# Column tiles for three groups of small products, and a new price for 64-column tile products in the order of issue

## The chip, the cores and the metric

The kernel runs on one core of one Trainium2 chip. The metric is the device time of one execution in microseconds (us). The kernel before took 1555.84 us, the median of three runs between 1552.79 and 1557.61. On this core five engines work side by side, each through its own list of instructions in a fixed order: TensorE (PE: products, with a weight load, PEld, ahead of each), VectorE (DVE), ScalarE (ACT), GpSimd (POOL) and SyncE (SP), which here only issues transfers (DMAs).

## The reference

One layer of a hybrid decoder is computed for a prompt of 1024 tokens and for 8 single-token samples with the same weights:

```
p = x @ w_in                                  # 1024 -> 9360 columns: GLA, RWKV and gate parts
GLA, 4 heads:   S_t = diag(a_t) S_(t-1) + k_t^T v_t ;   o_t = q_t S_t
RWKV, 16 heads: S_t = S_(t-1) (diag(w_t) - kk_t^T (kk_t a_t)) + v_t^T k_t ;   y_t = S_t r_t
m = sigmoid(gate_a) * (o_gla @ w_up_gla) + sigmoid(gate_b) * (o_rwkv @ w_up_rwkv)
y = layernorm(2^(1/4) x + m @ w_out)
```

The decay `w` and the rate `a` of the RWKV part come from small low-rank products (`rwkv_w2`, `rwkv_a2`, 64 rows each). Outputs are y, the new GLA and RWKV states and the last row before the token shift, for prompt and samples, all in float32.

## The kernel before

**Passes and tiles.** The prompt goes in two passes of 512 tokens; the 8 samples ride along with the first pass, as 8 further columns. Activations lie with their feature on the 128 partitions and their token along the free axis. The large products (`x @ w_in`, the two up-projections, the output) are made from a float32 value split into a high and a low part, so that each block of 128x128 weights costs three products (`xh,whi`, `xl,whi`, `xh,wlo` in the profile). All other products take float32 operands; the profile shows each of those as two matmul records on PE, the two passes of one float32 product (a group of four products is an "x8").

**Pairs and heads.** The 16 RWKV heads go two at a time (8 pairs a pass, function `pair`): `front` makes the factors and the Gram products (`pY<-az,wide` and `big<-az,wide`, 64x64 tiles), `back` completes a blockwise inverse from the tiles `Lp`, `As` and `Xs`, `turn` transposes, `chain` goes through 8 chunks and ends with two groups of 16 products into `pY`. The 4 GLA heads go one after the other (`gla_head`). In the first pass each head also does the samples (`gla_sample`): it loads the 8 states of 128x256 two at a time, updates them on ACT and DVE, stores them, and multiplies each with its sample's query, which stands in one column of an otherwise empty 8-column block (`qm`). `lora_sample` makes the low-rank products of the samples once, near the start.

**What sets the order.** Each such function is a stream of operations. `Order.run` takes, over and over, the operation with the smallest key: the time at which it could start by the planner's own account, less a bonus by the kind of stream (`ON_PE` for products, `PRIO` otherwise). That account adds up a price for each operation (`price`), 0.115 us where the tile shape on PE changes (`SWITCH`), and delays between engines. So a price in that table moves instructions of all engines, though no price is a time on the chip. `tiles` rounds the rows and columns of a product's weights up to 32, 64 or 128; `price` uses both. Everything is recorded through one helper, so that nearly all instructions carry line L219 in the profile, and groups are told apart by tile names and shapes.

**The lines around the change.** In `back` the two groups of 4 products read 128x128 weights and move 32 columns. In `gla_sample` there are 16 products a head, each with a 128x128 half of a state as weights and 8 moving columns:

```
yield self.P.matmul(po[:, j], Sg[:, w, j * P:(j + 1) * P], qm[:, NS * b:NS * b + NS],
                    start=(b == j == 0), stop=(b == NS - 1 and j == 1))
```

In `lora_sample` 4 products of 64 rows, 8 weight columns and 512 moving columns follow one another, each with its own load, bank of PSUM, copy and store. PSUM banks come from pools; `big` has three.

Of the kernel before, what the change touches and what calls it, by code (L numbers as in the profile page):

```python
# [76 lines left out]
PRIO = {"evacuate": 0.7, "pair": 0.4, "gram": 0.4, "turn": 0.5, "chain": 0.5, "norm": 0.1, "x": 0.7, "lora": 0.2, "rank": -0.3,  # L77
        "head": 0.3, "gate": 0.05, "w": 0.3, "out": -0.1, "state": 0, "block": 0.0}
ON_PE = {"evacuate": 0.0, "pair": 0.0, "gram": 0.16, "turn": 0.0, "chain": 0.0, "norm": 0.0, "x": 0.0, "lora": 0.175, "rank": 0.125,
# [67 lines left out]
def price(eng, name, out, args, ins):  # L147
# [3 lines left out]
    if eng == "P":  # L151
# [4 lines left out]
        if args[0].dtype == F32R:  # L156
            return max(m / 1200, n / 2200) if rows == P else (m + n) / 1200
        if rows == cols == P:
            return 2 * max(m, n) / 1200 + 0.005
        return 2 * max(m, n) / 1200 * rows * cols / P ** 2  # L160
# [252 lines left out]
class Kern(Order):  # L413
# [521 lines left out]
    def gla_sample(self, h, q, k, v, al, bufs, qm_):  # L935
# [12 lines left out]
        qm = qm_[:, :NS * NS]  # L948
        yield E.memset(qm, 0.0)
        yield E.tensor_copy(qm[:, ::NS + 1], q[:, HT:])  # L950
# [10 lines left out]
        po = yield from self.bank("big", [P, 2, NS])  # L961
        for n in range(NS // W):
            Sg, vb = (x[:, :W * GDV].rearrange("p (b v) -> p b v", b=W) for x in bufs[n % 2])
            for w in range(W):
                b = n * W + w
                t = HT + b
                yield A.activation(vb[:, w], vb[:, w], AF.Copy, scale=k[:, t:t + 1])
                yield V.scalar_tensor_tensor(Sg[:, w], Sg[:, w], al[:, t:t + 1], vb[:, w], ALU.mult, ALU.add)
                for j in range(2):
                    yield self.P.matmul(po[:, j], Sg[:, w, j * P:(j + 1) * P], qm[:, NS * b:NS * b + NS],  # L970
                                        start=(b == j == 0), stop=(b == NS - 1 and j == 1))
            yield self.S.dma_start(self.o["gla_s"][0, n * W:n * W + W, h].rearrange("b k v -> k b v"), Sg)
            if n + 2 < NS // W:
                yield from load(n + 2)
        for j in range(2):
            yield self.C.copy(v[j][:, HT:], po[:, j])
        self.free(po)
# [21 lines left out]
    def lora_sample(self, lw):  # L999
        for q in range(2):  # L1000
            rs = slice(64 * q, 64 * q + 64)
            for hf in range(2):
                l2, wa = yield from self.rows(2, 512)
                wa8 = wa[:NS]
# [202 lines left out]
    def back(self, d):  # L1207
# [10 lines left out]
        for y in range(NCH // 2):  # L1218
            yield self.P.matmul(pA[:, y], d.Lp[:, y], X1[:, y], start=True, stop=True)
# [554 lines left out]
```

## Time and profile before

| | |
|---|---|
| median of the runs | 1555.84 us (1552.79 to 1557.61) |
| the profiled execution | 1556.64 us, its span from first to last instruction 1554.9 us |
| instructions | 32217 |
| PE busy | 1510.2 us, 97% of the span |
| weight loads (PEld) busy | 1333.8 us, 86% |
| DVE, ACT, POOL busy | 1140.2 us (73%), 875.8 us (56%), 101.2 us (7%) |
| mean granted clock of PE | 0.988 |

A group of the profile is one line, engine, operation, pair of tile names and shape. `64*8` ahead of a matmul's shape are the rows and columns of its weights, and the last number before `f32` counts its moving columns. In a timeline the first column is the start, the second the time from the first start to the last end of the merged records. Matmul records overlap, since the next one enters while the last one still drains; what a product costs is therefore read from one start to the next, not from its own duration.

### The profile page before, as it was taken

What the parts mean: (1) busy time and instruction counts of PE and PEld (TensorE: products, weight loads), DVE (VectorE), ACT (ScalarE), POOL (GpSimd) and SP (SyncE); (2) the same over time, 40 slices, a digit from 0 to 9 for tenths busy, and PEclk for the clock granted to TensorE, in tenths of its full rate; (3) what the DMA queues carried; (4) which work ended last, traced back from release to release, by engine and by line L of the source; (5) the groups of instructions that cost most, each with busy time, mean ns of one, the idle gap of its engine ahead of it and who ended that gap; (6) DMA issues with size and microseconds to landing.
All of it is one profiled execution on the core that took longest, in us unless ns stands there. A gap on an engine that the chain in (4) does not pass through costs nothing.

```text
span 1554.9 us, 32217 instructions
## 1 busy us (share of the span) xinstructions
PE 1510.2 (97%) x11144; PEld 1333.8 (86%) x11144; DVE 1140.2 (73%) x3026; ACT 875.8 (56%) x2230; POOL 101.2 (7%) x208
## 2 busy tenths in 40 slices
PE   8999989999989999999999999999999999999998
PEld 8899979899989899788787778777887799988786
DVE  5695769785879678967877878787786784566665
ACT  5556566756676658664755474556445755554310
POOL 0100000100010001010100000102100000000000
PEclk9999979999999999999999999999999999999999
DMA  9878958678877787657557456855674687798622
GB/s 295 251 223 269 306 152 274 182 219 256 278 207 250 201 290 228 210 160 215 185 157 219 150 154 206 242 145 171 193 225 130 210 241 224 228 296 271 221 90 82
DMA packets 377055, 330.67 MB, mean 213 GB/s; under 512 B 131219, under 2 KB 262428, under 8 KB 376892
## 3 DMA queue, kind: packets, MB, share of 16 engines
q1 hardware_dynamic: 376892, 328.60, 69.7%
q8 instruction: 89, 1.46, 0.4%
q14 instruction: 74, 0.61, 0.1%
HBM read 198.35 MB, written 118.61 MB: 204 GB/s over the span
## 4 chain that ended last, share of the span: by engine, by line
PE 78%; DVE 11%; DMA 5%; ACT 3%; issue 2%; SPq 1%; POOL 0%; POOLq 0%; DVEq 0%; ACTq 0%
PE proj L219 47%; PE big L219 18%; PE pY L219 9%; DVE row L219 5%; PE pch L219 4%; ACT row L219 2%; DVE wide L219 1%; DVE Xt L219 1%; DVE X L219 1%; DMA S<-GS 1%; ACT L392 1%; SPq L219 1%; DMA wide<-LD 1%; DMA az<-wide 1%; DMA whi<-wh 1%
## 5 line engine op out<-in xcount | busy, mean ns | idle before, releaser
L219 PE MATMUL proj<-xh,whi 128*128 128x256 f32 (+2 forms) x1864 | 613.6, 329 | 2.9 <-ACT row L219 2.0
L219 PE MATMUL proj<-xh,wlo 128*128 128x256 f32 (+2 forms) x1864 | 612.4, 329 | 0.6 <-DMA wlo<-wl 0.5
L219 PE MATMUL proj<-xl,whi 128*128 128x256 f32 (+2 forms) x1864 | 612.7, 329 | 0.0
L219 PEld LDWEIGHTS proj<-xh,whi 128*128 128x128 f32 x1864 | 354.2, 190 | 25.4 <-ACT row L219 3.0
L219 PEld LDWEIGHTS proj<-xh,wlo 128*128 128x128 f32 x1864 | 354.6, 190 | 24.5 <-DMA wlo<-wl 1.8
L219 PEld LDWEIGHTS proj<-xl,whi 128*128 128x128 f32 x1864 | 354.4, 190 | 22.3 <-issue 2.2
L219 DVE TENSOR_TENSOR wlo<-wraw,whi 128x512 fp32r<-128x512 f32 x206 | 142.8, 694 | 75.7 <-ACT whi L219 73.6
L219 ACT CAST whi<-wraw 128x512 fp32r<-128x512 f32 x210 | 130.0, 621 | 76.6 <-PE proj L219 19.7
L219 DVE TENSOR_TENSOR row<-row 128x256 f32<-128x256 f32 (+9 forms) x328 | 158.1, 491 | 12.0 <-DMA row<-state_rwkv 3.7
L219 ACT ACTIVATE row<-row 128x512 f32<-128x512 f32 (+3 forms) x229 | 138.6, 611 | 30.9 <-DVE row L219 19.7
L219 DVE TENSOR_TENSOR Xt<-X,wide 128x60 f32<-128x60 f32 (+24 forms) x496 | 106.2, 214 | 23.2 <-DMA wide<-LD 10.6
L219 DVE TENSOR_TENSOR X<-X,Xt 128x60 f32<-128x60 f32 (+24 forms) x496 | 108.0, 218 | 12.5
L219 PE MATMUL big<-row 128*128 128x128 f32 (+3 forms) x530 | 99.7, 295 | 5.7 <-DVE row L219 5.1
L219 POOL TENSOR_TENSOR row<-row 128x512 f32<-128x512 f32 (+6 forms) x57 | 60.9, 1072 | 649.6 <-DVE row L219 296.7
L219 ACT COPY rh<-pch 128x128 f32<-128x128 f32 x114 | 30.5, 268 | 121.3 <-PE pch L219 120.6
L219 ACT ACTIVATE row<-proj,omu 128x256 f32<-128x256 f32 (+1 forms) x99 | 54.1, 547 | 75.1 <-PE proj L219 74.4
L219 DVE SCALAR_TENSOR_TENSOR row<-proj,pv,row 128x255 f32<-128x255 f32 (+1 forms) x99 | 56.5, 571 | 49.8 <-ACT tail L219 31.3
L219 DVE SCALAR_TENSOR_TENSOR wide<-pch,pc,s0p 64x64 f32<-64x64 f32 x224 | 63.1, 282 | 40.1 <-PE pch L219 34.7
L219 PEld LDWEIGHTS big<-row 128*128 128x128 f32 (+1 forms) x530 | 76.7, 192 | 16.3 <-DVE row L219 5.9
L219 ACT ACTIVATE s0p<-wide,pc 64x64 f32<-64x64 f32 x256 | 89.0, 348 | 2.0
L392 ACT ACT_TABLE_LOAD x56 | 71.8, 1283 | 1.0
L219 ACT COPY row<-big 128x128 f32<-128x128 f32 (+5 forms) x149 | 41.9, 303 | 47.1 <-PE big L219 45.9
(280 smaller groups left out, 2537.0 us busy)
## 6 DMA issues: line engine op xcount, KB each, us to landing
wraw<-w_in SPq DMA_DIRECT2D x146, 256.0 KB
wh<-whi SPq DMA_DIRECT2D x146, 256.0 KB
wl<-wlo SPq DMA_DIRECT2D x146, 256.0 KB
whi<-wh SPq DMA_DIRECT2D x146, 256.0 KB
wlo<-wl SPq DMA_DIRECT2D x146, 256.0 KB
wide<-LD SPq DMA_DIRECT2D x64, 128.0 KB
wraw<-w_up_gla SPq DMA_DIRECT2D x32, 256.0 KB
wraw<-w_up_rwkv SPq DMA_DIRECT2D x32, 256.0 KB
```

Source lines behind the costliest of these rows:

```text
L219: ways.append((eng, lambda call=call: call(out, *args, **kw), price(eng, name, out, args, ins)))
L392: self.nc.scalar.preload_act_table_set(self.table)
```

## The change

Three groups of products are rewritten so that they run in tiles of fewer weight columns that stand beside one another in the array, and the prices are changed.

- `back`: each product with 128x128 weights becomes two with 128x64 weights, one for each half of the output partitions. 4 products become 8, twice a pair, 16 pairs. The stream calls itself "gram" meanwhile (bonus 0.16 on PE, where "turn" has none).
- `gla_sample`: weights and moving operand change places. The weights are now 32 columns of `qm` (the sample's query and 31 zeros), the moving operand is a whole state of 256 columns. Four samples go to the four 32-partition quarters of one bank, in two groups a head, 8 products a head instead of 16. The result is the transpose of the one before, so it is copied out of PSUM, transposed by four products a head and copied again. The four state updates and both stores of a group now come before its products, and the second four samples are loaded after the first group's products, where before each two were replaced as soon as they were done.
- `lora_sample`: all loads come first, then the four products together, in two row halves and two column quarters and in two banks that are held at the same time; copies and stores follow.
- `price`: a float32 tile product with at most 64 moving columns is priced by the larger side of its tile and no longer by its area; a product of the split kind (float32r) with all 128 rows is priced in proportion to its weight columns, which lowers the price of the 32-column products at the start of each pass and of one 64-column block at the end. The bonuses have a new kind, "tiles".

```diff
--- before.py
+++ after.py
@@ -74,9 +74,9 @@
 BIAS = 0.1
 ASIDE = 0.5
 
-PRIO = {"evacuate": 0.7, "pair": 0.4, "gram": 0.4, "turn": 0.5, "chain": 0.5, "norm": 0.1, "x": 0.7, "lora": 0.2, "rank": -0.3,
+PRIO = {"evacuate": 0.7, "pair": 0.4, "gram": 0.4, "tiles": 0.3, "turn": 0.5, "chain": 0.5, "norm": 0.1, "x": 0.7, "lora": 0.2, "rank": -0.3,
         "head": 0.3, "gate": 0.05, "w": 0.3, "out": -0.1, "state": 0, "block": 0.0}
-ON_PE = {"evacuate": 0.0, "pair": 0.0, "gram": 0.16, "turn": 0.0, "chain": 0.0, "norm": 0.0, "x": 0.0, "lora": 0.175, "rank": 0.125,
+ON_PE = {"evacuate": 0.0, "pair": 0.0, "gram": 0.16, "tiles": 0.16, "turn": 0.0, "chain": 0.0, "norm": 0.0, "x": 0.0, "lora": 0.175, "rank": 0.125,
          "head": 0.1, "gate": 0.06, "w": 0.0, "out": -0.03, "state": 0.125, "block": 0.0}
 
 URGENT = 0.6
@@ -154,10 +154,10 @@
         if name == "transpose":
             return 0.112
         if args[0].dtype == F32R:
-            return max(m / 1200, n / 2200) if rows == P else (m + n) / 1200
+            return max(m / 1200, n / 2200) * cols / P if rows == P else (m + n) / 1200
         if rows == cols == P:
             return 2 * max(m, n) / 1200 + 0.005
-        return 2 * max(m, n) / 1200 * rows * cols / P ** 2
+        return 2 * max(m, n) / 1200 * (max(rows, cols) / P if n <= 64 else rows * cols / P ** 2)
     if eng == "S":
         return 0.48
     if eng == "A":
@@ -945,9 +945,9 @@
         yield self.S.dma_start(vd, vs)
         self.free(vs_)
 
-        qm = qm_[:, :NS * NS]
+        qm = qm_[:, :NS * 32]
         yield E.memset(qm, 0.0)
-        yield E.tensor_copy(qm[:, ::NS + 1], q[:, HT:])
+        yield E.tensor_copy(qm[:, ::32], q[:, HT:])
         W = 2
 
         def load(n):
@@ -958,23 +958,35 @@
             yield self.S.dma_start(vb[:, :W * GDV], vd[b].rearrange("b v -> (b v)").partition_broadcast(P))
         yield from load(0)
         yield from load(1)
-        po = yield from self.bank("big", [P, 2, NS])
-        for n in range(NS // W):
-            Sg, vb = (x[:, :W * GDV].rearrange("p (b v) -> p b v", b=W) for x in bufs[n % 2])
-            for w in range(W):
-                b = n * W + w
-                t = HT + b
-                yield A.activation(vb[:, w], vb[:, w], AF.Copy, scale=k[:, t:t + 1])
-                yield V.scalar_tensor_tensor(Sg[:, w], Sg[:, w], al[:, t:t + 1], vb[:, w], ALU.mult, ALU.add)
-                for j in range(2):
-                    yield self.P.matmul(po[:, j], Sg[:, w, j * P:(j + 1) * P], qm[:, NS * b:NS * b + NS],
-                                        start=(b == j == 0), stop=(b == NS - 1 and j == 1))
-            yield self.S.dma_start(self.o["gla_s"][0, n * W:n * W + W, h].rearrange("b k v -> k b v"), Sg)
-            if n + 2 < NS // W:
-                yield from load(n + 2)
+        po = yield from self.bank("big", [P, 2, GDV])
+        for g in range(2):
+            for n in range(2 * g, 2 * g + 2):
+                Sg, vb = (x[:, :W * GDV].rearrange("p (b v) -> p b v", b=W) for x in bufs[n % 2])
+                for w in range(W):
+                    t = HT + n * W + w
+                    yield A.activation(vb[:, w], vb[:, w], AF.Copy, scale=k[:, t:t + 1])
+                    yield V.scalar_tensor_tensor(Sg[:, w], Sg[:, w], al[:, t:t + 1], vb[:, w], ALU.mult, ALU.add)
+                yield self.S.dma_start(self.o["gla_s"][0, n * W:n * W + W, h].rearrange("b k v -> k b v"), Sg)
+            yield "tiles"
+            for c in range(4):
+                Sg = bufs[c // W][0][:, :W * GDV].rearrange("p (b v) -> p b v", b=W)
+                yield self.P.matmul(po[QS[c], g], qm[:, 32 * (4 * g + c):32 * (4 * g + c) + 32], Sg[:, c % W],
+                                    start=(g == 0), stop=(g == 1))
+            yield "head"
+            if g == 0:
+                yield from load(2)
+                yield from load(3)
+        os_ = yield from self.row(2 * GDV)
+        yield A.copy(os_, po.rearrange("p g v -> p (g v)"))
+        self.free(po)
+        pt = yield from self.bank("big", [P, 2, 2, P])
+        for g in range(2):
+            for j in range(2):
+                yield self.tr(pt[:, j, g], os_[:, g * GDV + j * P:g * GDV + (j + 1) * P])
+        self.free(os_)
         for j in range(2):
-            yield self.C.copy(v[j][:, HT:], po[:, j])
-        self.free(po)
+            yield self.C.copy(v[j][:, HT:].rearrange("p (g c) -> p g c", g=2), pt[:, j, :, ::32])
+        self.free(pt)
 
 
     def lora(self, c):
@@ -997,18 +1009,23 @@
         self.spawn(parts(), "lora")
 
     def lora_sample(self, lw):
+        l2 = yield from self.rows(2, 512)
+        for hf in range(2):
+            for q, rs in enumerate(HS):
+                yield self.S.dma_start(l2[hf][rs], self.a["lora2"][rs, q, 512 * hf:512 * hf + 512])
+        pw = [(yield from self.bank("big", [P, 512])), (yield from self.bank("big", [P, 512]))]
+        yield "tiles"
+        for hf in range(2):
+            for q, rs in enumerate(HS):
+                yield self.P.matmul(pw[q][32 * hf:32 * hf + NS], lw[rs, HT:], l2[hf][rs], start=True, stop=True)
+        yield "lora"
+        self.free(*l2)
         for q in range(2):
-            rs = slice(64 * q, 64 * q + 64)
+            wa = yield from self.row(2 * HT // 2)
             for hf in range(2):
-                l2, wa = yield from self.rows(2, 512)
-                wa8 = wa[:NS]
-                yield self.S.dma_start(l2[rs], self.a["lora2"][rs, q, 512 * hf:512 * hf + 512])
-                pw = yield from self.bank("big", [NS, 512])
-                yield self.P.matmul(pw, lw[rs, HT:], l2[rs], start=True, stop=True)
-                yield self.A.copy(wa8, pw)
-                self.free(l2, pw)
-                yield self.S.dma_start(self.WA[q, :, 512 * hf:512 * hf + 512], wa8)
-                self.free(wa)
+                yield self.A.copy(wa[32 * hf:32 * hf + NS], pw[q][32 * hf:32 * hf + NS])
+                yield self.S.dma_start(self.WA[q, :, 512 * hf:512 * hf + 512], wa[32 * hf:32 * hf + NS])
+            self.free(pw[q], wa)
 
     def tails(self):
         for j in range(3):
@@ -1215,14 +1232,20 @@
         X1, X2 = (d.Xs[:, n * P:(n + 1) * P].rearrange("p (y t) -> p y t", t=32) for n in (2, 1))
         yield self.V.transpose(d.Xs[:, 2 * P:3 * P], d.Xs[:, 0:P])
         pA = yield from self.bank("big", [P, NCH // 2, 32])
+        yield "gram"
         for y in range(NCH // 2):
-            yield self.P.matmul(pA[:, y], d.Lp[:, y], X1[:, y], start=True, stop=True)
+            for hs in HS:
+                yield self.P.matmul(pA[hs, y], d.Lp[:, y, hs], X1[:, y], start=True, stop=True)
+        yield "turn"
         for b in QS:
             yield self.C.copy(As[b, :, b], pA[b])
         self.free(pA, d.Lp)
         pZ = yield from self.bank("big", [P, NCH // 2, 32])
+        yield "gram"
         for y in range(NCH // 2):
-            yield self.P.matmul(pZ[:, y], As[:, y], X2[:, y], start=True, stop=True)
+            for hs in HS:
+                yield self.P.matmul(pZ[hs, y], As[:, y, hs], X2[:, y], start=True, stop=True)
+        yield "turn"
         for n, b in enumerate(QS):
             h = n % 2
             yield self.C.copy(XT[QS[2 * h], n // 2::2, h, 32:64], pZ[b])
```

The new prices move instructions from the start of the program on, on every engine; the numbers behind the tile names change with that. Three places on PE:

The first `back` of the program, on PE amid a projection. Before:

```order
L219 MATMUL proj<-xh_284,wlo 128x256
L219 MATMUL proj<-xh_293,whi 128x256
L219 MATMUL big<-Xs,Lp_173 128x32 x4
L219 MATMUL proj<-xl_304,whi 128x256
L219 MATMUL proj<-xh_293,wlo 128x256
```

Now:

```order
L219 MATMUL proj<-xh_290,whi 128x256
L219 MATMUL proj<-xl_302,whi 128x256
L219 MATMUL big<-Xs,Lp_173 64x32 x8
L219 MATMUL proj<-xh_290,wlo 128x256
L219 MATMUL proj<-xh_301,whi 128x256
```

The eight half products stand in one piece, here and at all 32 such places; the work on either side is the projection as before.

The samples of a GLA head, on PE: in the first head before, the products of one sample at a time,

```order
L219 MATMUL proj<-xh_284,whi 128x264
L219 MATMUL big<-row 128x8 x2
L219 MATMUL proj<-xl_294,whi 128x264
L219 MATMUL proj<-xh_284,wlo 128x264
L219 MATMUL proj<-xh_293,whi 128x264
L219 MATMUL proj<-xl_304,whi 128x264
L219 MATMUL proj<-xh_293,wlo 128x264
L219 MATMUL proj<-xh_187,whi 128x256
L219 MATMUL proj<-xl_207,whi 128x256
L219 MATMUL proj<-xh_187,wlo 128x256
L219 MATMUL big<-row 128x8 x2
```

and now its two groups, the first of them with a product of `chain` between, the second with the transposes behind it:

```order
L219 MATMUL proj<-xh_223,wlo 128x264
L219 MATMUL big<-row 32x256 x2
L219 MATMUL pch<-wide,gg 128x128
L219 MATMUL big<-row 32x256 x2
L219 MATMUL proj<-xh_239,whi 128x264
```

```order
L219 MATMUL proj<-xh_301,wlo 128x264
L219 MATMUL big<-part,headsr 128x512
L219 MATMUL big<-row 32x256 x4
L219 MATMUL big<-cons,row 128x128 x4
L219 MATMUL proj<-xh_187,whi 128x256
```

The other three heads have both groups in one piece, so 7 of 8 groups are.

The samples' low-rank products, on PE, four single places before, of which this is the first,

```order
L219 MATMUL proj<-xh_272,wlo 128x256
L219 MATMUL proj<-xh_284,whi 128x256
L219 MATMUL big<-row 8x512
L219 MATMUL proj<-xl_294,whi 128x256
L219 MATMUL proj<-xh_284,wlo 128x256
```

and now two places of two:

```order
L219 MATMUL proj<-xh_206,wlo 128x256
L219 MATMUL big<-row 8x512 x2
L219 MATMUL proj<-xh_223,whi 128x256
L219 MATMUL proj<-xl_241,whi 128x256
L219 MATMUL proj<-xh_223,wlo 128x256
L219 MATMUL proj<-xh_239,whi 128x256
L219 MATMUL big<-row 8x512 x2
L219 MATMUL proj<-xl_246,whi 128x256
```

The four products stand in two pairs, with four of the projection's products between them; each pair takes the two row halves of one column quarter.

## The prediction

> **What bounds the kernel now.** I read the page's head and its chain of work first, then the waits of PE, then the clock by stretches.
>
> ```profile
> span 1554.9 us, 32217 instructions
> PE 1510.2 (97%) x11144; PEld 1333.8 (86%) x11144; DVE 1140.2 (73%) x3026; ACT 875.8 (56%) x2230; POOL 101.2 (7%) x208
> PE 78%; DVE 11%; DMA 5%; ACT 3%; issue 2%; SPq 1%; POOL 0%; POOLq 0%; DVEq 0%; ACTq 0%
> ```
>
> PE is busy for 97% of the span and carries 78% of the chain that ended last; DVE, next, has a quarter of the span free. A microsecond taken off PE's own work should therefore come off the end nearly whole, as long as its list does not run into a wait instead. Its waits are few:
>
> ```profile
> PE big L219 <- DVE row L219: 6.3, 5, 2.7
> PE big L219 <- DVE part L219: 6.2, 4, 4.6
> PE big L219 <- ACT part L219: 5.0, 1, 5.0
> ```
>
> The two longest, 4.6 and 5.0 us, are one product each: a sum over a head (`headsr`) that stands in PE's list before DVE or ACT have split its operand. Their price is more than the wait:
>
> ```profile
> 195.00:220.00 25.00, 17.34 (x140) 14.94 (x139) 18.93 (x34) 14.24 (x30) 1.52 (x8) 0.71 0.64 182
> 430.00:450.00 20.00, 14.69 (x138) 12.80 (x137) 17.38 (x31) 13.44 (x25) 5.67 (x10) 0.83 0.87 237
> 450.00:1540.00 1090.00, 1072.25 (x7295) 916.77 (x7294) 799.55 (x2103) 599.67 (x1501) 69.03 (x128) 1.00 0.67 201
> ```
>
> The columns are the stretch, its length, busy time of PE, PEld, DVE, ACT and POOL, the granted clock, the DMA share and GB/s. In the first stretch PE is idle for 25 - 17.3 = 7.7 us and has lost 0.29 of its clock, 7.3 us of full speed; in the second 5.3 and 3.4 us. Part of the lost clock falls into the idle time, so these two places cost at most 15.0 and 8.7 us. From 450 to 1540 us the clock is 1.00 and PE idle for 1.6%.
>
> **The change part by part.** I cost each group by what it inserts between two products of the projection, from start to start, in one execution of 1556.64 us (span 1554.9).
>
> ```profile
> 139.56 0.29 PE L219 MATMUL proj<-xl,whi 128*128 128x264 f32 x1
> 139.69 0.97 PE L219 MATMUL big<-Xs,As 128*128 128x32 f32 x8
> 140.50 0.37 PE L219 MATMUL proj<-xh,wlo 128*128 128x264 f32 x1
> 140.70 0.28 PE L219 MATMUL proj<-xh,whi 128*128 128x264 f32 x1
> 140.82 0.29 PE L219 MATMUL proj<-xl,whi 128*128 128x264 f32 x1
> ...
> 154.39 0.28 PE L219 MATMUL proj<-xh,whi 128*128 128x264 f32 x1
> 154.51 0.51 PE L219 MATMUL big<-row 128*128 128x8 f32 x4
> 154.87 0.37 PE L219 MATMUL proj<-xl,whi 128*128 128x264 f32 x1
> 155.08 0.28 PE L219 MATMUL proj<-xh,wlo 128*128 128x264 f32 x1
> ```
>
> Between two undisturbed projection products lie 140.82 - 140.70 = 0.12 us. From 139.56 to 140.70 are 1.14 us, less two such steps 0.90: a `back` group costs 0.90 us, 0.112 a pass. From 154.39 to 155.08, 0.69 - 0.24 = 0.45 us: two sample products cost 0.45 us, 0.112 a pass too. Passes with 128 weight columns cost the same whether they move 32 columns or 8: they are bound by their weights.
>
> What narrower tiles cost, three rows show:
>
> ```profile
> 192.50 1.15 PE L219 MATMUL pY<-gg,az 128*64 128x64 f32 x32
> ...
> L219 PE MATMUL pY<-gg,az 128*64 128x64 f32 x512 | 18.4, 225 | 0.0
> ...
> 66.65 0.28 PE L219 MATMUL proj<-xl,whi 128*128 128x256 f32 x1
> 67.13 0.27 PE L219 MATMUL big<-az,wide 64*64 64x128 f32 x1
> 67.13 0.27 PE L219 MATMUL pY<-az,wide 64*64 64x128 f32 x1
> 67.14 0.27 PE L219 MATMUL big<-az,wide 64*64 64x128 f32 x1
> 67.15 0.27 PE L219 MATMUL pY<-az,wide 64*64 64x128 f32 x1
> 67.23 0.27 PE L219 MATMUL big<-az,wide 64*64 64x128 f32 x1
> 67.89 0.39 PE L219 MATMUL proj<-xh,wlo 128*128 128x256 f32 x1
> 68.11 0.28 PE L219 MATMUL proj<-xh,whi 128*128 128x256 f32 x1
> ...
> 32.63 0.28 PE L219 MATMUL proj<-xh,whi 128*128 128x256 f32 x1
> 32.84 1.02 PE L219 MATMUL big<-row 64*8 64x512 f32 x2
> 33.79 0.38 PE L219 MATMUL proj<-xl,whi 128*128 128x256 f32 x1
> 34.02 0.28 PE L219 MATMUL proj<-xh,wlo 128*128 128x256 f32 x1
> ...
> L219 PE MATMUL big<-row 64*8 64x512 f32 x8 | 4.1, 591 | 0.0
> ```
>
> In the 128x64 form that `back` is to get, 32 passes start within 1.15 - 0.225 = 0.93 us, one each 0.93/31 = 0.030 us, 0.060 within each of two tiles. In the Gram products four passes of 128 columns, one per tile, start together and the next four 0.10 to 0.11 us later: four tiles run at four times the rate of one. The low-rank pair: 34.02 - 32.63 - 0.24 = 1.15 us, where one pass of 512 columns takes 1.02 - 0.59 = 0.43, so 0.86 are passes and 0.29 the change of tile shape on both sides. For the Gram group (32 passes, 8 steps of 0.11) it is 68.11 - 66.65 - 0.24 = 1.22, less 0.88: 0.34. I take 0.31 us for leaving and taking up the full array.
>
> `back`: now 16 passes at 0.030 plus 0.31 = 0.79 us, before 0.90. Over 32 groups **-3.5 us**. Bounds: if two tiles did not overlap in this form, a pass would cost 0.060 and a group 1.27 (+11.8 us); if a pass of 32 columns went at half the time of one of 64, 0.55 (-11.2 us). The pY row has the same weights, so I stay with it.
>
> The Trainium skill speaks against this part: "TensorEngine Tiling (Array Packing)", section Performance Considerations, says that each matmul carries an overhead of about 60 cycles and that a tiling factor should not be taken from a dimension that is already small. The pY row agrees with no such cost per pass of the list, since two tiles share it.
>
> `gla_sample`: it removes 64 products, 128 passes at 0.112 = 14.3 us. It adds 8 groups of four 32-column tiles, each moving 256 columns twice. A pass of 256 is half of 0.43, 0.215 us; with four at a time a group is 0.43 + 0.31 = 0.74 us, eight are 5.9. The one group that the order splits around a `pch` product pays the passes and the shape change twice, +0.74. Sixteen transposes are one pass each, about 0.11, 1.8 us. Together 8.4, **-5.9 us**. No row shows four streams of 128 rows each; the Gram tiles move four of 64. Bounds: no overlap, 64 x 0.215 + 9 x 0.31 + 1.8 = 18.4 us (+4.1); no shape change seen, 5.2 (-9.1). I take the Gram rate, the only four-tile row.
>
> The Trainium skill, "TensorE: Matmul & The Clock Gate", Part 3, gives 2.38 times for three column tiles and 3.07 for four row tiles. By 3.07 instead of 4 the eight groups would take about 1.0 us longer; the trace's Gram tiles do better than that.
>
> `lora_sample`: before 4 x 1.15 = 4.6 us; now two pairs, each with its two row halves side by side, 2 x 1.15 = 2.3: **-2.3 us**. Bounds: no overlap, 4 x 0.86 + 2 x 0.29 = 4.0 (-0.6).
>
> What lies beside other work I cost at nothing. Each head's extra copy of 512 columns and its two small ones go to ACT and DVE, 56% and 73% busy. The samples' states now come in two batches, the second only when the first group's products and both stores are through; its loads stand in SP's list behind those stores.
>
> ```profile
> L219 SPq DMA_DIRECT2D gla_s<-row x16: 388/428/1267, 162.0 to 736.0; - x16
> L219 SPq DMA_DIRECT2D row<-o_gla x16: 376/430/932, 1221.1 to 1342.4; - x16
> ```
>
> The last sample state is stored at 736 us and the GLA result first read at 1221: 485 us of projection lie between, and heads of the second pass wait in line behind the first's. What is late next, if that cover were gone, is the next head, and with it the bank that `gla_sample` keeps. The two banks of `lora_sample`, held near 33 us, are two of three in `big`; the sums and decays that want one then are behind them. I see no wait of PE for a bank there and take 0.
>
> **The prices** have no sum. The two groups into `pY` are now priced at twice the amount, the low-rank ones at a quarter, and all lists are dealt anew. I take 0 and bound it by the two costly places above: up to 15 + 8.7 = 23.7 us either way.
>
> The sum is -3.5 - 5.9 - 2.3 = -11.7 us: 1556.64 - 11.7 = 1544.9 for the profiled execution. That execution lies 0.8 us over the median of the runs, so **1544 us**.
>
> **Rivals.**
>
> *PE outruns its feeders.* For a pair's 32 pY products the planner added 16 x 0.027 + 16 x 0.053 = 1.3 us, now 2.6; the trace has about 2 x 1.15 = 2.3. With its half products of `back` too (16 x 0.107 = 1.7 for two groups, plus shape changes, where the rows give 1.6 with them), the planner holds PE for later than it is. Sums over a head then stand too early in PE's list, and it waits at `headsr`, as at 201.7 and 436 us. For: those are the longest waits, and each drags the clock down. Against: DVE and ACT have room to run ahead. It decides against the change from 11.7 + 4.7 = 16.4 us of further stall; a second pair of such places gives 1544 + 23.7 = 1568.
>
> *The new order loses the costly place instead.* Nothing in the program demands a stall at 201 us: ACT and DVE were just behind there. Without it 1544 - 15 = 1529. For: prices nearer the trace's 2.3 us than before. Against: that other places may come up as well.
>
> *The tiles do not overlap* in 128x64 with 32 columns and in 128x32: +11.8 + 4.1 - 0.6 = +15.3, 1571. Against: the pY row, which shows the first nearly as it will be. With only the 128x32 form failing, 1544 + 10.0 = 1554: the change would do what it says and save almost nothing.
>
> **How the numbers follow.** Forecast 0.55, PE outrunning its feeders 0.18, the costly place gone 0.17, tiles that do not overlap 0.10 (mostly in the 128x32 form alone). What a measurement of this kernel can tell from no change is about 0.3%, 4.7 us: faster is below 1551.2, slower above 1560.5. Within the forecast, small waits that move leave 1535 to 1554, so I give it 0.43 faster and 0.12 the same; the first rival 0.13 slower and 0.05 the same; the second 0.17 faster; the third 0.06 the same and 0.04 slower. Together 0.60, 0.23, 0.17. The range takes in the place that goes and part of the stalls that come: 1528 to 1562; the forecast's own is 1535 to 1554.
>
> **What would show it.** Right: the 128x8 group is gone from PE; a `back` group inserts about 0.8 us between two projection products; the four passes of a samples' group start within some 0.02 us of each other, and the group inserts about 0.75; PE's waits stay near those of before. Wrong: passes that start one after another; waits at `headsr` longer than 5 us, or stretches with a clock of 0.8 and less at new places; a span that moves by more than these groups do, which would be the order's doing and not the tiles'.

## The result, and the profile after

| | before | after |
|---|---|---|
| median of the runs | 1552.79 us (5 runs beside the change) | 1539.91 us (5 runs, 1537.94 to 1545.27) |
| ratio after / before, 95% interval | | 0.9911 [0.9888, 0.9935] |
| the profiled execution | 1556.64 us, span 1554.9 us | 1537.94 us, span 1536.1 us |
| mean granted clock of PE | 0.988 | 0.995 |

The change makes the kernel faster by 0.89%, which is 13.8 us [10.1, 17.4] of some 1554. Forecast were 11.7 us less and 1544 us; of the 4 us between 1544 and 1539.91, 3 are the kernel before, whose runs beside the change had a median of 1552.79 us instead of 1555.84. The profiled execution of before lay at the upper end of its runs and that of after is the fastest of its own, so the two traces lie 18.7 us apart; the ratio is what counts.

The head of the page of after:

```profile
span 1536.1 us, 32633 instructions
PE 1492.0 (97%) x11352; PEld 1304.9 (85%) x11352; DVE 1146.4 (75%) x3044; ACT 866.7 (56%) x2218; POOL 87.3 (6%) x202
```

PE's busy time fell by 1510.2 - 1492.0 = 18.2 us, its idle time hardly: 1554.9 - 1510.2 = 44.7 us before, 44.1 us now. The clock that was not granted is 0.012 x 1554.9 = 18.7 us before and 0.005 x 1536.1 = 7.7 us now. So up to 11.0 of the 18.2 us can be products that ran at full instead of half speed, and at least 7.2 are work that is gone. The sum of the three groups, 11.7, lies between.

The waits of PE after, in the columns of the prediction (total us, times, longest):

```profile
PE big L219 <- DVE part L219: 6.1, 4, 2.5
PE big L219 <- ACT row L219: 5.6, 4, 4.2
```

The longest wait of a sum over a head was 4.6 us on DVE and 5.0 us on ACT; it is now 2.5 us. The wait of 4.2 us on ACT is new. The stretches of the prediction again, after:

```profile
195.00:220.00 25.00, 18.72 (x197) 16.20 (x197) 19.03 (x30) 17.50 (x41) 2.66 (x9) 0.86 0.62 168
430.00:450.00 20.00, 19.91 (x217) 17.55 (x216) 17.53 (x30) 15.04 (x38) 0.85 (x8) 1.00 0.67 192
450.00:1520.00 1070.00, 1046.78 (x7294) 884.24 (x7293) 789.75 (x2063) 574.26 (x1442) 55.23 (x118) 1.00 0.68 203
```

The costly place at 430 us is gone: PE is idle for 0.1 us there, where it was 5.3, and the clock is whole. The one at 200 us is still there, with 6.3 us idle instead of 7.7 and a clock of 0.86 instead of 0.71. From 450 us on PE is idle for 23.2 us of 1070, where it was 17.8 of 1090: what the two places gave, later ones took back in part.

The three groups of products. First their rows in the profile of before,

```profile
L219 PE MATMUL big<-row 128*128 128x8 f32 x128 | 17.5, 245 | 2.7 <-DVE row L219 2.7
L219 PE MATMUL big<-Xs,Lp 128*128 128x32 f32 x128 | 17.5, 280 | 1.0 <-DVE Xs L219 1.0
```

then of after:

```profile
L219 PE MATMUL big<-Xs,Lp 128*64 128x32 f32 x256 | 10.8, 225 | 0.6 <-DVE row L219 0.4 <-DVE Xs L219 0.2
L219 PE MATMUL big<-row 128*32 128x256 f32 x64 | 6.2, 391 | 0.0
```

The 128x8 group is gone from the list of after, and the counts are what the change says. What a group costs is read from the starts around it, in PE's timeline of after: a low-rank pair, a `back` group and a samples' group.

```profile
35.02 0.28 PE L219 MATMUL proj<-xh,wlo 128*128 128x256 f32 x1
35.23 1.03 PE L219 MATMUL big<-row 64*8 64x512 f32 x4
36.19 0.39 PE L219 MATMUL proj<-xh,whi 128*128 128x256 f32 x1
36.41 0.28 PE L219 MATMUL proj<-xl,whi 128*128 128x256 f32 x1
...
132.56 0.28 PE L219 MATMUL proj<-xl,whi 128*128 128x256 f32 x1
132.77 0.66 PE L219 MATMUL big<-Xs,Lp 128*64 128x32 f32 x16
133.36 0.39 PE L219 MATMUL proj<-xh,wlo 128*128 128x256 f32 x1
133.58 0.28 PE L219 MATMUL proj<-xh,whi 128*128 128x256 f32 x1
...
314.84 0.28 PE L219 MATMUL proj<-xh,whi 128*128 128x264 f32 x1
315.06 0.64 PE L219 MATMUL big<-row 128*32 128x256 f32 x8
315.63 0.49 PE L219 MATMUL pch<-wide,gg 128*128 128x128 f32 x2
315.87 0.37 PE L219 MATMUL proj<-xl,whi 128*128 128x264 f32 x1
316.07 0.28 PE L219 MATMUL proj<-xh,wlo 128*128 128x264 f32 x1
```

By the prediction's own rule, less two projection steps of 0.12 us:

- A low-rank pair: 36.41 - 35.02 - 0.24 = 1.15 us for two products, where one took 1.15 before. Predicted 1.15.
- A `back` group: 133.58 - 132.56 - 0.24 = 0.78 us. Predicted 0.79; before 0.90.
- A samples' group: 316.07 - 314.84 - 0.24 = 0.99, less about 0.22 for the two `pch` passes (two at 0.112), 0.77 us. Predicted 0.74. The eight passes take 0.64 us from the first start to the last end, one alone 0.391 by its group's row, so all eight start within about 0.25 us; in the trace the first four start within 0.02 us of each other, as the prediction asked, and the second four 0.24 us after the first. One after another at 0.215 they would need 7 x 0.215 = 1.5 us: four run at once.

The Trainium skill, "TensorE: Matmul & The Clock Gate", Part 3, gives 3.07 times for four row tiles. By that figure a samples' group would take, as an estimate, 0.13 us more than the predicted 0.74, so some 1.0 us for the eight groups; the group of the trace, at 0.77, lies nearer to the full four.

### The profile page after: what moved, and what is told of

Read it like the earlier page. It is cut to its first block, busy times and chain, and to the rows that moved or that the text cites. A ratio compares the mean times of both kernels' runs of the same rounds, so it can differ in the third digit from the quotient of the medians.

```text
span 1536.1 us, 32633 instructions
## 1 busy us (share of the span) xinstructions
PE 1492.0 (97%) x11352; PEld 1304.9 (85%) x11352; DVE 1146.4 (75%) x3044; ACT 866.7 (56%) x2218; POOL 87.3 (6%) x202
## 5 line engine op out<-in xcount | busy, mean ns | idle before, releaser
L219 PE MATMUL proj<-xh,whi 128*128 128x264 f32 (+2 forms) x1880 | 618.3, 329 | 5.9 <-ACT whi L219 2.7
L219 PE MATMUL proj<-xh,wlo 128*128 128x264 f32 (+2 forms) x1880 | 617.7, 329 | 0.3 <-DVE wlo L219 0.2
L219 PE MATMUL proj<-xl,whi 128*128 128x264 f32 (+2 forms) x1880 | 617.7, 329 | 0.0
L219 DVE TENSOR_TENSOR row<-row 128x256 f32<-128x256 f32 (+8 forms) x330 | 165.2, 509 | 20.1 <-DMA row<-state_rwkv 6.7
L219 DVE TENSOR_TENSOR X<-X,Xt 128x60 f32<-128x60 f32 (+24 forms) x496 | 104.7, 211 | 12.2
L219 PE MATMUL big<-row 128*128 128x128 f32 (+4 forms) x466 | 87.0, 323 | 5.9 <-DVE row L219 4.2
L219 POOL TENSOR_TENSOR row<-row 128x256 f32<-128x256 f32 (+7 forms) x55 | 49.5, 904 | 573.4 <-DVE row L219 313.2
L219 DVE SCALAR_TENSOR_TENSOR wide<-pch,pc,s0p 64x64 f32<-64x64 f32 x224 | 63.0, 281 | 22.8 <-PE pch L219 18.8
L219 PEld LDWEIGHTS big<-row 128*128 128x128 f32 (+3 forms) x466 | 59.0, 179 | 17.5 <-ACT row L219 6.2
```

Of the source, the lines that this page charges most:

```text
L219: ways.append((eng, lambda call=call: call(out, *args, **kw), price(eng, name, out, args, ins)))
```

## Experiments

Two questions were open: whether the saving seen between starts comes off the end, and what the new order of all lists is worth. In the expectations the theories go by letters: T puts the gain to the narrower tiles, O to the order that the new prices deal, P holds that truer prices deal better orders, N that the quality of an order has little to do with how true the prices are, S that PE's idle time in a stall is lost for good, with the clock behind it where the stall is long, R that later waits shrink and make up for a stall. Each ratio is against the kernel before on the same chip; a difference of ratios is turned into time at 1554 us. Where two ratios are compared, their intervals together come to 4 to 6 us either way.

### One group at a time, in an order that is held

To leave the order alone, the planner still prices and places the operations of the parent kernel, and only what an operation emits is exchanged. All other instructions on all engines stand as in the parent.

**The order of before, with half products in `back`** (shown for the first of its two groups):

```diff
-            yield self.P.matmul(pA[:, y], d.Lp[:, y], X1[:, y], start=True, stop=True)
+            op = self.P.matmul(pA[:, y], d.Lp[:, y], X1[:, y], start=True, stop=True)
+            yield self.instead(op, lambda y=y: [self.nc.tensor.matmul(
+                pA[hs, y], d.Lp[:, y, hs], X1[:, y], start=True, stop=True) for hs in HS])
...
```

> The kernel before in its own order, instruction for instruction, with the half products of back issued where the full ones stood. Theory T (the tiles' saving is PE's own and holds in any order): 32 x 0.11 = 3.5 us under the kernel before, ratio 0.998. Theory O (what a saving on PE is worth depends on the order): within 1 us of the kernel before.

Measured: 1551.33 us, 0.9963 [0.9947, 0.9979], so 5.7 us less [3.3, 8.2]. The page's head of this kernel:

```profile
span 1551.7 us, 32733 instructions
PE 1505.5 (97%) x11400; PEld 1320.0 (85%) x11400; DVE 1138.9 (73%) x3026; ACT 876.3 (56%) x2230; POOL 102.5 (7%) x208
```

and its two costly places:

```profile
195.00:220.00 25.00, 17.33 (x158) 14.85 (x157) 19.62 (x35) 15.00 (x32) 1.52 (x8) 0.73 0.64 182
430.00:450.00 20.00, 14.97 (x166) 12.90 (x164) 16.49 (x30) 12.97 (x29) 5.68 (x10) 0.83 0.76 204
```

Both places stand as before (17.34 and 14.69 us busy, clock 0.71 and 0.83), and the mean clock is 0.987, where it was 0.988. So this gain owes nothing to those two places: PE's busy time fell by 1510.2 - 1505.5 = 4.7 us. The spans of these two single executions lie 3.2 us apart, the runs of the two kernels 5.7 us. What PE saves comes off the end, within the spread of the runs: T held.

**The order of after, with full products in `back`** (again the first group; the second half product emits nothing):

```diff
             for hs in HS:
-                yield self.P.matmul(pA[hs, y], d.Lp[:, y, hs], X1[:, y], start=True, stop=True)
+                op = self.P.matmul(pA[hs, y], d.Lp[:, y, hs], X1[:, y], start=True, stop=True)
+                yield self.instead(op, lambda y=y, hs=hs: hs == LO and self.nc.tensor.matmul(
+                    pA[:, y], d.Lp[:, y], X1[:, y], start=True, stop=True))
...
```

> The changed kernel in its own order, instruction for instruction, but the 32 groups of back are full 128x128 products again, issued where the half products stood. This takes the order out of the comparison. T: a group inserts 0.90 us again where the half products insert 0.79, 32 x 0.11 = 3.5 us over the changed kernel, 1543.4. O: no more than 1 us over it, since PE's saving there would end in waits.

Measured: 1546.02 us, 0.9946 [0.9928, 0.9964]. That is 0.0035 +- 0.0030 over after, 5.4 +- 4.6 us. The size agrees with the first experiment, but here the mean clock of the profiled executions fell too, from 0.995 to 0.993, so a part of it is not the passes themselves. The interval starts at 0.8 us, so this run alone hardly rules out the 1 us of O.

**The order of after, with the old products in `gla_sample`**: sixteen products with the state as weights, small copies, and neither transposes nor a wide copy.

```diff
-                yield self.P.matmul(po[QS[c], g], qm[:, 32 * (4 * g + c):32 * (4 * g + c) + 32], Sg[:, c % W], ...)
+                op = self.P.matmul(po[QS[c], g], qm[:, 32 * (4 * g + c):32 * (4 * g + c) + 32], Sg[:, c % W], ...)
+                yield self.instead(op, lambda b=4 * g + c, x=Sg[:, c % W]: [self.nc.tensor.matmul(
+                    po8[:, j], x[:, j * P:(j + 1) * P], qm[:, 31 * b:31 * b + NS],
+                    start=(b == j == 0), stop=(b == NS - 1 and j == 1)) for j in range(2)])
...
-                yield self.tr(pt[:, j, g], os_[:, g * GDV + j * P:g * GDV + (j + 1) * P])
+                op = self.tr(pt[:, j, g], os_[:, g * GDV + j * P:g * GDV + (j + 1) * P])
+                yield self.instead(op, (lambda: [self.nc.scalar.copy(v[x][:, HT:], os_[:, x * NS:x * NS + NS])
+                                                 for x in range(2)]) if g == j == 1 else lambda: None)
```

> The changed kernel in its own order, but each samples' group of a head issues the sixteen old products with the state as weights (two for each of the tile products, at the same places), and the four transposes and the wide copy are left out. T: 14.3 us of passes in place of the 8.4 that the tiles and the transposes were reckoned to take, so 5.9 us over the changed kernel, 1545.8. O: no more than 2 us over it.

Measured: 1546.52 us, 0.9954 [0.9939, 0.9969], which is 0.0043 +- 0.0028 over after, 6.7 +- 4.4 us; predicted were 5.9, so T held. It also answers for the new wait of 4.2 us. Around it PE's timeline of after reads

```profile
198.19 0.64 PE L219 MATMUL big<-row 128*32 128x256 f32 x8
203.07 1.12 PE L219 MATMUL big<-cons,row 128*128 128x128 f32 x4 [4.23 <-ACT row L219]
205.43 0.58 PE L219 MATMUL proj<-xh,whi 128*128 128x256 f32 x1 [1.24 <-ACT row L219]
```

and that of this experiment

```profile
198.23 1.85 PE L976 MATMUL big<-row 128*128 128x8 f32 x16
204.39 0.58 PE L219 MATMUL proj<-xh,whi 128*128 128x256 f32 x1 [4.31 <-ACT row L219]
```

In after the transposes wait for ACT, then the next product of the projection waits for it again, and the projection goes on at 205.43. Without the transposes that product waits 4.31 us for ACT at the same place, and the projection goes on at 204.39. Most of the stall is ACT being behind there; about 1 us of it goes with the wide copy and the transposes.

### The order

**The changed kernel at the old prices** (both lines of `price` as before):

> The three groups in column tiles as changed, with the prices of before. Theory T (the tiles' own saving of 11.7 us on PE is the gain, and what the new prices do to the order is worth about nothing): 11 to 12 us under the kernel before, so about 1541, give or take 5 us of chance in the order. Theory O (most of the gain came with the new order: the stall near 201 us that is shorter and the clock that was lost behind it): within 5 us of the kernel before.

**The kernel before at the new prices** (the same two lines, nothing else):

> The kernel before with nothing but the new prices. T: as before, 1553, give or take 5 us. O: 7 us or more under the kernel before, with the long waits at the sums over a head gone.

Measured: 0.9951 [0.9932, 0.9970] and 1.0153 [1.0125, 1.0180]. So the new prices are worth 6 us with the new products and cost 24 us with the old ones. The first kernel is 7.6 us [4.7, 10.6] under the kernel before, within T's 11 to 12 give or take 5 and hardly clear of the 5 that O allowed. The second is slower, where T saw no change and O a gain: neither theory had this. Waits of PE in the slow one:

```profile
PE proj L219 <- DVE row L219: 9.2, 3, 7.1
L219 PE MATMUL big<-row 128*128 128x8 f32 x128 | 19.5, 261 | 6.4 <-DVE row L219 6.4
L219 PE MATMUL big<-part,headsr 128*128 128x512 f32 x128 | 57.0, 453 | 6.3 <-DVE part L219 3.5 <-ACT part L219 1.5 <-POOL part L219 0.8
```

One wait of 7.1 us for DVE stands in front of a projection. The old samples' products, each of which needs a state that DVE has just updated, wait for 6.4 us, where it was 2.7. The sums over a head (`headsr`) wait less than before: 6.3 us, where the prediction's rows have 6.2 and 5.0.

**One price line undone, each in turn:**

```diff
-            return max(m / 1200, n / 2200) * cols / P if rows == P else (m + n) / 1200
+            return max(m / 1200, n / 2200) if rows == P else (m + n) / 1200
```

> The changed kernel without the lower price for products of the split kind in narrow tiles; the price by the larger side stays. Theory P (a price that is nearer to what the trace shows deals a better order): the rows of the 32-column products start to start are those of full ones, so the lower price is wrong, and undoing it gains, 1530 to 1538. Theory N (each new set of prices deals a new order, and how good that is has little to do with how true the prices are): anywhere from 1530 to 1560, with no sign given.

```diff
-        return 2 * max(m, n) / 1200 * (max(rows, cols) / P if n <= 64 else rows * cols / P ** 2)
+        return 2 * max(m, n) / 1200 * rows * cols / P ** 2
```

> The changed kernel with the area price for products that move up to 64 columns; the lower price of the split kind stays. P: the pY products then are priced at 1.3 us where the trace has 2.3, and the order is worse, 1545 to 1552. N: anywhere from 1530 to 1560.

Measured: 0.9957 [0.9942, 0.9971] and 1.0048 [1.0030, 1.0066]. Over after, taking back the split price costs 7 us, the price for 64 moving columns 21 us, and both together (0.9951, above) only 6. The effects of the two lines don't add up; each setting deals an order of its own. P had the sign wrong for the first line; for the second it had the sign, but 1559.9 us lies beyond its 1552. In the slower one, as at the old prices, a sum over a head waits long for ACT again, which is the 6.7 us here:

```profile
PE big L219 <- ACT part L219: 7.2, 2, 6.7
```

**An edit that says nothing about the work**: the planner's constant for a change of tile shape, 4% up.

```diff
-SWITCH = 0.115
+SWITCH = 0.12
```

> The changed kernel with the planner's price for a change of tile shape at 0.12 us in place of 0.115, and nothing else. P: the two prices are equally far from the 0.31 us that the trace shows for two changes, so the time stays within 3 us of the changed kernel's, 1537 to 1543. N: as far away as the other two, 5 us and more either way in half of such cases.

**Prices as the traces have them**: 0.06 us a product for up to 64 moving columns, four times the price for the low-rank pair.

```diff
-        return 2 * max(m, n) / 1200 * (max(rows, cols) / P if n <= 64 else rows * cols / P ** 2)
+        return 0.06 if n <= 64 else 2 * max(m, n) / 1200 * rows * cols / P ** 2 * (4 if n == 512 else 1)
```

(with the old line for the split products)

> The changed kernel with prices as the trace has them start to start: 0.06 us for a tile product of up to 64 columns, 0.43 for the samples' low-rank products, the full price for split products in narrow tiles. P: the best order of all, 1527 to 1537. N: anywhere from 1530 to 1560.

**A wider margin in the planner**, `SPARE` 0.8 instead of 0.4:

> The changed kernel with 0.8 us in place of 0.4 as the planner's margin between DVE, ACT or GpSimd and a product that reads their result, and nothing else. If the orders differ by how often PE runs into operands that are not there yet, a larger margin makes for fewer and shorter waits at the sums over a head, a clock of 0.995 or more, and 1525 to 1538. If the planner's account is too coarse for that, anywhere from 1530 to 1560.

Measured: 0.9951 [0.9929, 0.9974], 1.0075 [1.0046, 1.0105] and 1.0078 [1.0058, 1.0098]. The small constant alone moved 6.2 +- 5.1 us, where P allowed 3; the two others lie at 1563.7 and 1568.2 us, beyond even the 1560 that N and the doubt about the margin allowed. In the profile of the small constant neither of the two costly places is left:

```profile
195.00:220.00 25.00, 24.75 (x245) 22.61 (x247) 20.63 (x35) 19.88 (x44) 4.51 (x5) 1.00 0.90 266
430.00:450.00 20.00, 19.64 (x186) 17.29 (x184) 17.13 (x32) 15.16 (x37) 0.61 (x3) 1.00 0.70 197
```

It is nevertheless slower than after; other waits have come up, such as these two of up to 3.9 and 4.2 us:

```profile
PE big L219 <- DMA S<-GS: 5.9, 3, 3.9
PE big L219 <- DVE Xs L219: 4.7, 3, 4.2
```

The prices that are nearest to the trace gave one of the slowest orders. PE's waits there,

```profile
PE big L219 <- DVE part L219: 12.7, 6, 9.5
PE big L219 <- ACT part L219: 10.8, 4, 7.2
```

and under the wider margin:

```profile
PE big L219 <- DVE Xs L219: 8.4, 3, 3.3
```

Each order has a few long waits, on other engines and at other places each time. Put together, with the same products in tiles:

| order | median, us | ratio to before | profiled span, us | mean clock | PE busy, us |
|---|---|---|---|---|---|
| the change | 1539.91 | 0.9911 | 1536.1 | 0.995 | 1492.0 |
| other constant | 1545.28 | 0.9951 | 1543.2 | 0.993 | 1495.0 |
| split price undone | 1546.51 | 0.9957 | 1544.4 | 0.991 | 1496.1 |
| old prices | 1547.65 | 0.9951 | 1549.6 | 0.988 | 1495.7 |
| 64-column price undone | 1559.88 | 1.0048 | 1556.4 | 0.985 | 1501.6 |
| measured prices | 1563.66 | 1.0075 | 1560.5 | 0.983 | 1499.6 |
| wider margin | 1568.20 | 1.0078 | 1570.1 | 0.981 | 1506.8 |

Seven orders of the same products spread over 0.0167, 26 us, nearly twice what the change brings. PE's busy time differs by 15 us among them and the span by 34; these are single executions, that of the change the fastest of its runs, those of the old prices and of the wider margin the slowest of theirs. In them the span goes with the clock from the first row to the last. Between those two rows PE's idle time grows from 44.1 to 63.3 us and the clock that was not granted from 7.7 to 29.8 us, a part of it within the idle time. So the difference is stalls, and the half-speed work behind them. P fell: neither truer prices nor more margin gave a better order. O was wrong for the gain as a whole, since two of the three groups save their time in held orders, but right that an order alone can move more than they do.

### The price of a stall

Four stalls were put into after, its order held: in every second pair of the second pass, ahead of the pair's first transpose in `turn`, PE has to wait until POOL has cleared a small buffer ten times in the first kernel and 24 times in the second. Nothing that the outputs depend on is touched.

```diff
+                if c.i and not p % 2 and not x and not n:
+                    def late(fn=op.fn, q=pt[:, 0, 0:8], z=self.zz):
+                        self.nc.tensor.matmul(q, z[:, :P], z[:, :8], start=True, stop=True)
+                        for _ in range(10):
+                            self.nc.gpsimd.memset(z, 0.0)
+                        self.nc.tensor.matmul(q, z[:, :P], z[:, :8], start=True, stop=True)
+                        fn()
```

> The changed kernel in its own order, with four extra stalls of PE in the second pass, at the first transposes of every other pair: PE makes a small product from a spare tile, GpSimd clears that tile ten times, PE makes the product again. A stall of some 1 to 3 us each. Theory S (PE is the bound, and an idle microsecond of PE is lost for good): the sum of the four stalls over the changed kernel, 4 to 12 us. Theory R (work behind the stall is then ready sooner, so later waits shrink): less than half of the stalls' sum.

> As the short stalls, with 24 clearings each, so stalls of 3 to 7 us, about the length of those at 201 and 436 us in the kernel before. S: the four stalls' sum, and on top of it the clock that is lost behind each (half speed for 3.4 to 6.8 us, as behind the two long waits of before, 2 to 3 us each): 20 to 40 us over the changed kernel. R: less than the idle time that was added.

Measured: 1.0030 [1.0013, 1.0048] and 1.0154 [1.0130, 1.0177]; over after 0.0119 and 0.0243, so 18.5 and 37.8 us. The stalls themselves (three of the four in each kernel; the fourth is as long as the others), with ten clearings,

```profile
PE big L1272 <- POOL row L219: 8.1, 3, 2.7
```

and with 24:

```profile
PE big L1272 <- POOL row L219: 19.1, 3, 6.4
```

Four stalls of 2.7 us are 10.8 us idle and cost 18.5 +- 4.6 us; four of 6.4 us are 25.5 us and cost 37.8 +- 5.2. The 16 passes of the eight extra products are about 1.8 us of either, as an estimate at 0.112 us a pass. The rest of what comes on top stands behind the stalls. The stretch around the first stall, in after, with 2.7 us and with 6.4 us:

```profile
735.00:760.00 25.00, 24.67 (x188) 19.69 (x188) 19.56 (x38) 18.47 (x43) 0.00 (x0) 1.00 0.62 173
```

```profile
735.00:760.00 25.00, 21.96 (x132) 17.36 (x135) 16.52 (x32) 17.25 (x33) 2.77 (x16) 0.86 0.56 157
```

```profile
735.00:760.00 25.00, 18.28 (x105) 14.46 (x105) 13.38 (x26) 14.73 (x30) 5.64 (x30) 0.80 0.47 120
```

The clock loses 0.14 x 25 = 3.5 us with the stall of 2.7 us and 5.0 us with the one of 6.4, a part of it while PE is idle. In PE's timeline around the longer one

```profile
735.83 0.39 PE L219 MATMUL proj<-xh,whi 128*128 128x512 f32 x1
736.06 0.39 PE L219 MATMUL proj<-xl,whi 128*128 128x512 f32 x1
...
747.50 0.63 PE L219 MATMUL proj<-xl,whi 128*128 128x512 f32 x1
747.93 0.63 PE L219 MATMUL proj<-xh,wlo 128*128 128x512 f32 x1
```

projection products come 0.43 us apart behind the stall; ahead of it the same products came every 0.23. Behind the second short stall, which ends at 893.97, half speed lasts for 3.41 us (the columns are the stretch, its length, PE's busy time, the granted clock, the DMA share and GB/s):

```profile
890.88:894.29 3.41, 0.72 (x7) 1.00 0.05 19
894.29:897.71 3.42, 3.42 (x13) 0.50 0.25 71
897.71:901.12 3.41, 3.26 (x24) 1.00 0.41 95
```

The four short stalls bring 6.8, 3.4, 6.8 and 3.4 us at half speed, the four long ones 10.2, 10.2, 6.8 and 6.8, which begin while PE is still idle. PE is busy for 18.3 us of the former and 18.4 us of the latter, so about 9.2 us of full speed are lost by either set. The sums, 10.8 + 9.1 + 1.8 = 21.7 and 25.5 + 9.2 + 1.8 = 36.5 us, lie within the measured 18.5 +- 4.6 and 37.8 +- 5.2. So a stall costs its length and some 2.3 us of clock behind it, here as much for 2.7 as for 6.4 us; it is no multiple of its length.

In the kernel with short stalls the profile, of the slowest of its ten runs, also shows a wait of PE for DVE of 4.4 us that after does not have. R fell. For the long stalls S held, 20 to 40 us; for the short ones it had counted the idle time alone, 4 to 12 us, and missed the clock.

## Why the prediction was right, step by step

**PE bounds the kernel.** Right. The span of the two traces fell by 18.8 us, PE's busy time by 18.2.

**`back`, -3.5 us.** Right in its mechanism: two 128x64 tiles share the array, and a group inserts 0.78 us for 0.79 predicted. Off the end came 5.7 us [3.3, 8.2] in the old order and 5.4 +- 4.6 in the new; the term was, if anything, too small. It was costed from groups that stand alone in a projection; whether a group that stands beside other tile products pays for the change of shape was not measured.

**`gla_sample`, -5.9 us.** Right: 6.7 +- 4.4 in the held order, 0.77 us a group for 0.74. Taking the rate of the only four-tile row, though each of its tiles moved 64 rows and not 128, was the choice that held. The transposes' 1.8 us were not measured by themselves.

**`lora_sample`, -2.3 us.** A pair inserts 1.15 us as predicted; no run had it alone.

**Copies, banks and loads at nothing.** Right to about 1 us. DVE is busy 6.2 us more, ACT 9.1 less. Of the two longer new waits for ACT the one at 203 us is there without the wide copy and the transposes too, shorter by some 1 us; the other, 2.7 us for the weights `whi` at 1278 us, long after the samples, stays without them too (3.0 us) and so belongs to the order.

**The prices at 0, bounded by 23.7 us.** This is the term that was right by luck. The change measured 13.8 us less, the three groups come to 5.7 + 6.7 + 2.3 = 14.7 by the held orders and the trace, and so some +1 is left for the order, if the savings add up. It is uncertain by about 3 us, since after's own time drops out of that sum: what is compared is the old order with halves in `back` against the new order with the old samples' products, 0.9963 and 0.9954. By the same account the order of the changed kernel at the old prices costs some 7 us (14.7 against its 7.6), and the new prices win 6 of them back. So its being near 0 is no property of the prices: on the old products the same two lines cost 24 us, and six neighbouring settings of the new kernel lie 6 to 26 us over this one. That the setting of the change is the fastest of the seven may be chance or the choice of whoever set it; no run tells. Reading the bound off the two costly places gave about the right size, 23.7 beside a spread of 26. The weight on it was too small: with the kernel before at 1555.84 us, the two slowest orders of seven come to 1567.5 and 1568.0, over the range's upper end of 1562.

**PE outruns its feeders.** Not seen. The longest wait of a sum over a head went from 5.0 to 2.5 us. Nor did the mechanism show where it should: with the old products the new prices made the sums wait less (6.3 us), and waits of a sum of 6.7 and 9.5 us stand in kernels whose pY products are priced lower than in the change. One of these, with the old price for 64 columns, is slower than the change by 21 us.

**The costly place gone.** Half of it happened. The place at 430 us went (up to 8.7 us), the one at 200 us lost 1.4 us of idle time and 3.8 of lost clock, and PE waits 5.4 us more from 450 us on. What was named against this rival, that other places may come up, is what took its gain. The kernel with the other constant shows the same more plainly: it has neither place, and is slower.

**Tiles that do not overlap.** Out, by the starts.

## What to carry to other kernels

Price a change of tile shape from start to start in the trace, change of shape included, and it will hold to some hundredths of a microsecond a group; the end follows, within the few microseconds that runs differ by, where one engine is busy for 97%. Where a scheduler deals all lists anew, a change in its prices acts like a draw, so measure the spread with a few neighbouring settings (here seven orders over 26 us, and 6 +- 5 us from the one edit that means nothing) before a gain of 14 us is put to the products, and hold the order to see what the products alone are worth. Prices nearer the chip did not deal better orders; what separates the orders is the few long stalls and the half-speed work behind them, some 2.3 us a stall here on top of its length.

## What the runs showed of the hardware that was not expected

All four stalls of 2.7 us lost the clock. The Trainium skill, "TensorE: Matmul & The Clock Gate", Part 1, has the clock fall after an idle window of about 3.4 us. By that, no stall of 2.7 us would lose it; the length agrees with the traces here, the need of a wholly idle window does not. In the fourteen traces every piece at half speed away from start and end lasts a multiple of 3.41 us, and all pieces of a trace lie on one beat of that length. What counts is how long PE is busy within one such piece. Two stalls of after, in the columns of the short stall above:

```profile
813.10:816.51 3.41, 0.46 (x2) 1.00 1.10 224
816.51:819.93 3.42, 3.06 (x31) 0.50 0.11 32
...
1273.89:1277.31 3.42, 1.57 (x13) 1.00 1.13 305
1277.31:1280.72 3.41, 2.37 (x17) 1.00 1.13 314
```

The first, 2.39 us ahead of a sum over a head, leaves PE busy for 0.46 us of its piece, and the next piece runs at half speed. The second, 2.65 us, is split over two pieces, and no clock is lost. Over all fourteen traces, 56 of 56 pieces at full speed with PE busy for less than 45% were followed by half speed, 20 of the 52 between 45 and 66%, and none of the 6007 above. On this kernel, then, where a stall falls on the beat decides as much as its length.

Four 32-column tiles, each with a moving operand of its own of 128 rows, ran at nearly the full rate of four: the second four passes of 256 columns started 0.24 us after the first, where one pass takes 0.215.
